# First residual formed during the scan and kept in HBM, second norm's scale and shift applied on ScalarE's evictions, and its residual added in the last stage

## The chip, the cores and the metric

One core of a Trainium2 chip runs the whole program in one launch. TensorE (PE), VectorE (DVE), ScalarE (ACT) and GpSimd (POOL) each work through a queue of their own in a fixed order; SyncE (SP) issues most of the DMAs. The metric is the device time of one execution in microseconds.

## What is computed

One layer of an encoder over 1024 positions of 1024 channels, in float32. A norm of x gives h. A projection of h feeds four mixers of 256 channels each: a state-space scan (S5), a matrix-state recurrence run forwards and backwards (RWKV-7), a gated convolution and a two-dimensional Fourier mixer. Their outputs are concatenated and projected, and two residuals with norms close the layer:

```
h = layer_norm(x, ln0_g, ln0_b)
mix = concat(s5(h), rwkv7(h), conv(h), fourier(h)) @ w_out
h = layer_norm(ALPHA * h + mix, ln1_g, ln1_b)
f = (silu(h @ w1) * (h @ w3)) @ w2
out = layer_norm(ALPHA * h + f, ln2_g, ln2_b)          # ALPHA = 2 ** 0.25
```

## The kernel before

Positions are eight tiles of 128, numbered 7 to 0 in the order in which they are worked on. Large products are made as three (`mm3`): each operand is split into a rounded upper part and the remainder, a cast on ScalarE and a subtraction on VectorE or GpSimd (`split_to`). `Tile` pools hand out buffers by tag, and a planner sets the order of each engine's queue from priorities and estimated times; an engine then takes its queue strictly in that order.

The stages, with their times in the profile: the first norm, the projection, S5 and the convolution (to about 440 us), with the preparation of the recurrence. `rk_scan` then makes 32 steps, 16 forwards and 16 backwards (about 497 to 675 us). Each direction needs the inverse of triangular blocks (`rk_inverse`): a loop of multiplications and sums that VectorE and GpSimd share by heads (L1174, L1176), then transposes and small products. The backward inverse runs beside the forward steps and has to be through before the first backward solve. A step of the scan goes through TensorE several times: transposes `pt`, products `px`, `pz`, `po` and `pc`, with ScalarE and VectorE evicting in between; L1321 is VectorE's update of the state, once in a step, and L1268 GpSimd's two copies for the step. Beside the steps stand the Fourier mixer (`fourier`, its table products `fpa` and `fpb` for each of two halves), `out_weights`, which loads the eight row blocks of w_out as `oraw` and splits them into `owa`, `owb`, `owc` (L1397 on VectorE, L1398 on GpSimd), and `rk_out`, which closes a tile of the recurrence (transposes `pgn`).

The output projection follows: for each tile t, `residual` loads x, subtracts the first norm's mean and multiplies by its deviation (L1432, VectorE), multiplies by ALPHA times the norm's scale row (L1434, GpSimd) and adds ALPHA times its shift row (L1435, VectorE), all 128x1024. `out_load` loads the mixers' output `yraw` from `d_y` and splits it; the products `ops` go through `out_product`, 48 for a tile, and L1455 adds them to the residual. `norm` makes the statistics (L172 and the lines to L187) and two instructions with the scale and shift rows (L1465, L1466). `turn` transposes two tiles (`ot`), evicts with two copies a tile (L1519), scales the tile by ALPHA on ScalarE (L1520), stores it in `d_acc`, and forms the sums and splits `H` that the feed-forward part's fast matrix scheme wants (L1528 to L1535, L1385). The first product of the feed-forward part (`fx`, `fy`, `fz`) runs from about 775 to 1238 us; weights are loaded, split and combined on the fly. The second (`ff_second`, products `f`) takes 924 products in seven groups to 1452 us; behind the fourth group (n == 3) it loads `d_acc` and adds it (L1782, L1783). `ff_out` makes the last norm.

Of the kernel before, what the change touches and what calls it, by code (L numbers as in the profile page):

```python
# [46 lines left out]
def pack(inp):  # L47
# [36 lines left out]
    for d, (m_in, m_st) in enumerate(((lo, st), (lo.T, st.T))):  # L84
# [5 lines left out]
        "x": f(a["x"][0]), "vec": f(vec), "rows": f(rows), "w_in": f(w_in), "lora": f(lora),  # L90
# [49 lines left out]
class Trunk:  # L140
# [72 lines left out]
    def build(self):  # L213
        tc = self.tc
        with tc.tile_pool(name="const", bufs=1) as cp, tc.tile_pool(name="dram", bufs=1, space=DRAM) as dp, \
# [4 lines left out]
            with tc.tile_pool(name="m", bufs=1) as m, tc.tile_pool(name="mp", bufs=1, space=PSUM) as pp:  # L220
                self.m, self.pp = m, pp
                with ExitStack() as pools:
# [3 lines left out]
                    def beside():  # L226
                        for part in (self.lora_project, self.rkv_project, self.conv, self.fourier_project):
                            yield from part()
                        self.far = [self.hp.tile([128, 4096], F32, tag=tag, name=tag + "f") for tag in ("HA0", "HB0", "HA1", "HB1")]
                        yield from self.until(("rows", 1, 1))  # L230
                        yield from self.first(self.rwkv_second(), 200000)
                        self.done.add("inverse")
                        yield from self.until("scan0")
                        yield from woven((self.fourier(), 0), (self.out_weights(), 32))
                        yield from self.out_first()
# [29 lines left out]
    def consts(self, cp):  # L265
# [37 lines left out]

        self.d_acc = self.dp.tile([8, 128, D], F32, name="d_acc")
# [675 lines left out]
    def rwkv_second(self):  # L980
# [3 lines left out]
        for c in (slice(8, 16), slice(0, 8)):  # L984
            for p in range(2):
                for i, dst in enumerate((self.av[1], self.bk[1])):
                    nc.sync.dma_start(out=dst[:, p, c], in_=self.d_p[p, i, :, c])
# [419 lines left out]


    def out_first(self):
        nc = self.nc  # L1410
        rows = self.t("TT", [128, 4, D], "rows")
        self.row4 = [rows[:, i] for i in range(4)]
        for i in range(4):
            self.row_load(rows[:, i], i)
        for i in range(2):
            nc.scalar.mul(out=rows[:, i], in_=rows[:, i], mul=ALPHA)
# [10 lines left out]

    def residual(self, t, tag):
        nc = self.nc
        ht = self.acc[t] = self.t(tag, [128, D], "acc")  # L1430
        nc.sync.dma_start(out=ht, in_=self.A["x"][t * 128:(t + 1) * 128, :])
        nc.vector.tensor_scalar(out=ht, in0=ht, scalar1=self.st0[:, t, 0:1], scalar2=self.st0[:, t, 1:2],  # L1432
                                op0=ALU.subtract, op1=ALU.mult)
        nc.gpsimd.tensor_tensor(out=ht, in0=ht, in1=self.row4[0], op=ALU.mult)  # L1434
        nc.vector.tensor_tensor(out=ht, in0=ht, in1=self.row4[1], op=ALU.add)  # L1435

    def out_load(self, t):
# [3 lines left out]
        self.split_to(*self.y_parts(t), raw, nc.vector if t > 5 else None)  # L1441
# [15 lines left out]
    def out_proj(self):  # L1457
        nc = self.nc
        g1, b1 = self.row4[2:]
        self.raws = ["WR", "T7"]  # L1460

        def norm(t):
            ht = self.acc[t]
            mean, rstd = self.row_stats(self.m, ht, D, LN_EPS)
            nc.vector.scalar_tensor_tensor(out=ht, in0=ht, scalar=mean, in1=g1, op0=ALU.subtract, op1=ALU.mult)  # L1465
            nc.vector.scalar_tensor_tensor(out=ht, in0=ht, scalar=rstd, in1=b1, op0=ALU.mult, op1=ALU.add)  # L1466
# [40 lines left out]
    def turn(self, j, tags):  # L1507
# [4 lines left out]
        for t, dst in ((7 - 2 * j, (b11, b21)), (6 - 2 * j, (b12, b22))):  # L1512
            ht = self.acc[t]
            for q in range(2):
# [4 lines left out]
                nc.scalar.copy(out=dst[q], in_=ps)  # L1519
            nc.scalar.mul(out=ht, in_=ht, mul=ALPHA)  # L1520
            nc.sync.dma_start(out=self.d_acc[t], in_=ht)
# [146 lines left out]
    def ff_second(self):  # L1668
# [9 lines left out]
        self.row_load(self.g2, 4)  # L1678
        self.row_load(self.b2, 5)
# [85 lines left out]
        for n in range(6):  # L1765
# [13 lines left out]
            if n == 3:  # L1779
                for t in range(NT - 1, -1, -1):  # L1780
                    x = self.ring("x", [128, D])
                    nc.sync.dma_start(out=x, in_=self.d_acc[t])  # L1782
                    tt(out=self.acc[t], in0=self.acc[t], in1=x, op=ALU.add)  # L1783

# [57 lines left out]
```

## Time and profile before

| | us |
|---|---|
| median of 3 runs | 1463.02 |
| runs | 1460.07 to 1464.85 |
| profiled execution | 1465.01 |
| its span | 1462.2 |
| granted TensorE clock, mean | 0.958 |

The profile is one execution. Its page gives busy times by engine over the whole span; the windows give them by stretch, and the chain of waits tells what released what. A busy TensorE is not TensorE at its peak. The prediction is made for the median; the profiled execution is 2.0 us above it.

### The profile page before, as it was taken

The numbers are of one execution on the slowest core, as the hardware profiler recorded it, in microseconds if no ns is written. First come the engines' busy times: TensorE is split into PE (matmuls) and PEld (weight loads), VectorE is DVE, ScalarE is ACT, GpSimd is POOL, SyncE is SP. The second block draws the span as 40 slices with busy tenths as digits, with TensorE's granted clock in tenths as the row PEclk, the third lists the DMA queues.
The fourth block names the chain that finished last, engine by engine and source line by source line (L and its number), as shares of the span: only waits on it lengthen the run. The fifth ranks groups of instructions, "written<-read, shape, count | busy, mean of one in ns | idle before, by whom it ended". The sixth has DMA issues, their size and how long they took to land.

```text
span 1462.2 us, 23749 instructions
## 1 busy us (share of the span) xinstructions
PE 1323.2 (90%) x9072; PEld 1196.4 (82%) x9072; DVE 1100.0 (75%) x1910; ACT 621.7 (43%) x1205; POOL 575.7 (39%) x524
## 2 busy tenths in 40 slices
PE   6968797977797999999877899999999999999997
PEld 5968787766796787877766899999999999888885
DVE  8997966487997685779999866666676665346888
ACT  4312141656324785761426544444444444332231
POOL 6466663153574332325567633333333331000006
PEclk9989998999899898999999899999999999999999
DMA  6111033122325004244312434444444438996752
GB/s 241 49 54 29 13 94 87 44 70 89 87 73 180 2 15 148 84 128 154 118 70 87 138 123 159 147 147 143 157 147 142 150 137 291 385 315 234 273 188 115
DMA packets 97056, 193.95 MB, mean 133 GB/s; under 512 B 24624, under 2 KB 50864, under 8 KB 96944
## 3 DMA queue, kind: packets, MB, share of 16 engines
q1 hardware_dynamic: 94912, 187.59, 38.3%
q10 hardware_dynamic: 2032, 4.86, 1.0%
q8 instruction: 71, 1.16, 0.3%
q14 instruction: 41, 0.34, 0.1%
HBM read 127.41 MB, written 63.96 MB: 131 GB/s over the span
## 4 chain that ended last, share of the span: by engine, by line
PE 42%; DVE 12%; DMA 3%; issue 2%; ACT 1%; POOL 1%; DVEq 0%; SPq 0%; ACTq 0%; POOLq 0%
PE fx L160 5%; PE fx L162 5%; PE fx L161 5%; PE f L160 4%; PE f L162 4%; PE f L161 4%; PE fy L162 2%; PE fy L160 2%; PE fy L161 2%; DVE acc L1435 1%; PE fz L160 1%; PE fz L161 1%; PE fz L162 1%; DMA fw<-w 1%; PE ops L161 1%
## 5 line engine op out<-in xcount | busy, mean ns | idle before, releaser
L160 PE MATMUL proj<-HA,wh 128*128 128x256 f32 x672 | 195.5, 291 | 14.6 <-DVE la L919 11.8
L160 PE MATMUL fx<-H,fc 128*128 128x256 f32 x704 | 196.9, 284 | 5.7 <-ACT fc L1384 2.2
L161 PE MATMUL proj<-HB,wh 128*128 128x256 f32 x672 | 200.1, 298 | 1.7 <-POOL HB L334 1.7
L162 PE MATMUL proj<-HA,wl 128*128 128x256 f32 x672 | 196.6, 293 | 4.1 <-POOL wl L394 4.1
L162 PE MATMUL fx<-H,fc 128*128 128x256 f32 x704 | 197.8, 282 | 2.6 <-DVE fc L1385 2.6
L1385 POOL TENSOR_TENSOR fc<-fw,fc 128x512 fp32r<-128x512 f32 x96 | 137.3, 1432 | 158.5 <-ACT fc L1384 157.7
L161 PE MATMUL fx<-H,fc 128*128 128x256 f32 x704 | 198.5, 282 | 0.0
L160 PEld LDWEIGHTS proj<-HA,wh 128*128 128x128 f32 x672 | 131.8, 196 | 18.4 <-issue 7.7
L162 PEld LDWEIGHTS proj<-HA,wl 128*128 128x128 f32 x672 | 131.5, 196 | 10.0 <-issue 5.5
L160 PEld LDWEIGHTS fx<-H,fc 128*128 128x128 f32 x704 | 132.5, 190 | 7.8 <-ACT fe L1633 2.7
L161 PEld LDWEIGHTS proj<-HB,wh 128*128 128x128 f32 x672 | 131.5, 196 | 7.0 <-issue 4.8
L162 PEld LDWEIGHTS fx<-H,fc 128*128 128x128 f32 x704 | 133.7, 191 | 2.8 <-DVE fc L1385 2.8
L161 PEld LDWEIGHTS fx<-H,fc 128*128 128x128 f32 x704 | 134.1, 191 | 0.1
L160 PE MATMUL f<-fb,fa 128*128 128x512 f32 x276 | 108.9, 395 | 0.0
L162 PE MATMUL f<-fb,fa 128*128 128x512 f32 x276 | 108.9, 394 | 0.0
L161 PE MATMUL f<-fb,fa 128*128 128x512 f32 x276 | 108.7, 394 | 0.0
L160 PE MATMUL fy<-H,fc 128*128 128x256 f32 x352 | 100.0, 284 | 4.7 <-ACT fe L1642 3.6
L162 PE MATMUL fy<-H,fc 128*128 128x256 f32 x352 | 99.5, 284 | 0.2 <-DVE fc L1385 0.2
L161 PE MATMUL fy<-H,fc 128*128 128x256 f32 x352 | 99.5, 283 | 0.0
L1821 POOL TENSOR_TENSOR acc<-acc,g 128x1024 f32<-128x1024 f32 x4 | 11.6, 2904 | 205.8 <-ACT acc L1820 205.8
L1384 ACT CAST fc<-fw 128x512 fp32r<-128x512 f32 x120 | 73.7, 619 | 31.8 <-POOL fc L1385 15.7
L1385 POOL TENSOR_TENSOR fc<-fs,fc 128x512 fp32r<-128x512 f32 x24 | 33.4, 1391 | 119.4 <-ACT fc L1384 116.0
(602 smaller groups left out, 3761.6 us busy)
## 6 DMA issues: line engine op xcount, KB each, us to landing
fa<-d_f SPq DMA_DIRECT2D x77, 512.0 KB, 3.8
d_f<-fg SPq DMA_DIRECT2D x70, 512.0 KB, 2.9
fw<-w SPq DMA_DIRECT2D x48, 512.0 KB, 3.6
fg<-w SPq DMA_DIRECT2D x44, 256.0 KB, 5.3
wraw<-w_in SPq DMA_DIRECT2D x16, 512.0 KB, 4.0
xt<-x SPq DMA_DIRECT2D x8, 512.0 KB, 8.1
oraw<-w_out SPq DMA_DIRECT2D x8, 512.0 KB, 3.7
yraw<-d_y SPq DMA_DIRECT2D x8, 512.0 KB, 4.1
```

Of the source, the lines that this page charges most:

```text
L160: mm(out, whi, xhi, start=start, stop=False, skip_group_check=shared)
L161: mm(out, whi, xlo, start=False, stop=False, skip_group_check=shared)
L162: mm(out, wlo, xhi, start=False, stop=stop, skip_group_check=shared)
L1384: nc.scalar.copy(out=hi, in_=raw)
L1385: (eng or nc.gpsimd).tensor_tensor(out=lo, in0=raw, in1=hi.bitcast(F32), op=ALU.subtract)
L1435: nc.vector.tensor_tensor(out=ht, in0=ht, in1=self.row4[1], op=ALU.add)
L1821: nc.gpsimd.tensor_tensor(out=o, in0=o, in1=self.g2, op=ALU.mult)
```

## The change

`residual` is cut to one load. A new generator, `residuals`, makes the same values for tiles 7 to 0 during the scan, woven with `fourier` and `out_weights`: it loads and scales the two rows on ScalarE's queue, then for each tile loads x on SP into the one buffer Z2, applies mean and deviation on ScalarE (Identity with scale and bias), multiplies and adds the rows on GpSimd and stores the tile in `d_res`. `issue_after` puts the first load behind the last of the loads by which the recurrence's rows return (L987).

`norm` becomes one VectorE instruction (subtract the mean, multiply by the deviation), and the tile is stored in `d_acc` from there, unscaled. `turn` evicts each 128x128 block by itself on ScalarE, with scale and shift per partition from `vec1`, and no longer scales the tile. In `ff_second` the rows g2 and b2 first hold ALPHA times the second norm's rows; behind the second group (n == 1) the normalized tile is loaded, multiplied by g2 on GpSimd, and it and b2 are added on VectorE; then the last norm's rows are loaded into the same buffers. The adds behind n == 3 go. The lower part of `yraw` is always made on VectorE, where GpSimd made it for six tiles.

```diff
-                        yield from woven((self.fourier(), 0), (self.out_weights(), 32))
+                        yield from woven((self.fourier(), 0), (self.residuals(), 0), (self.out_weights(), 32))
...
-                    nc.sync.dma_start(out=dst[:, p, c], in_=self.d_p[p, i, :, c])
+                    self.back = nc.sync.dma_start(out=dst[:, p, c], in_=self.d_p[p, i, :, c])
...
+    def alpha_row(self, out, i):
+        self.row_load(out, i)
+        self.nc.scalar.mul(out=out, in_=out, mul=ALPHA)
...
-        rows = self.t("TT", [128, 4, D], "rows")
-        self.row4 = [rows[:, i] for i in range(4)]
-        for i in range(4):
-            self.row_load(rows[:, i], i)
-        for i in range(2):
-            nc.scalar.mul(out=rows[:, i], in_=rows[:, i], mul=ALPHA)
...
+    def residuals(self):
+        nc = self.nc
+        g0, b0 = (self.t(f"Z{i}", [128, D], "row") for i in range(2))
+        self.alpha_row(g0, 0)
+        self.alpha_row(b0, 1)
...
+        for t in range(NT - 1, -1, -1):
+            x = self.t("Z2", [128, D], "res")
+
+            with self.tc.issue_after(self.back.ins):
+                nc.sync.dma_start(out=x, in_=self.A["x"][t * 128:(t + 1) * 128, :])
+            nc.scalar.activation(out=x, in_=x, func=AF.Identity, scale=self.st0[:, t, 1:2], bias=nm0[:, t:t + 1])
+            nc.gpsimd.tensor_tensor(out=x, in0=x, in1=g0, op=ALU.mult)
+            nc.gpsimd.tensor_tensor(out=x, in0=x, in1=b0, op=ALU.add)
+            nc.sync.dma_start(out=self.d_res[t], in_=x)
+            yield 8
+
     def residual(self, t, tag):
...
-        nc.sync.dma_start(out=ht, in_=self.A["x"][t * 128:(t + 1) * 128, :])
-        nc.vector.tensor_scalar(out=ht, in0=ht, scalar1=self.st0[:, t, 0:1], scalar2=self.st0[:, t, 1:2],
-                                op0=ALU.subtract, op1=ALU.mult)
-        nc.gpsimd.tensor_tensor(out=ht, in0=ht, in1=self.row4[0], op=ALU.mult)
-        nc.vector.tensor_tensor(out=ht, in0=ht, in1=self.row4[1], op=ALU.add)
+        self.acc[t] = self.t(tag, [128, D], "acc")
+        self.nc.sync.dma_start(out=self.acc[t], in_=self.d_res[t])
...
-        self.split_to(*self.y_parts(t), raw, nc.vector if t > 5 else None)
+        self.split_to(*self.y_parts(t), raw, nc.vector)
...
-            nc.vector.scalar_tensor_tensor(out=ht, in0=ht, scalar=mean, in1=g1, op0=ALU.subtract, op1=ALU.mult)
-            nc.vector.scalar_tensor_tensor(out=ht, in0=ht, scalar=rstd, in1=b1, op0=ALU.mult, op1=ALU.add)
+            nc.vector.tensor_scalar(out=ht, in0=ht, scalar1=mean, scalar2=rstd, op0=ALU.subtract, op1=ALU.mult)
+            nc.sync.dma_start(out=self.d_acc[t], in_=ht)
...
-                nc.scalar.copy(out=dst[q], in_=ps)
-            nc.scalar.mul(out=ht, in_=ht, mul=ALPHA)
-            nc.sync.dma_start(out=self.d_acc[t], in_=ht)
+
+                for k in range(4):
+                    nc.scalar.activation(out=dst[q][:, k], in_=ps[:, k, :], func=AF.Identity,
+                                         scale=self.vec1[:, 4 * q + k:4 * q + k + 1],
+                                         bias=self.vec1[:, 8 + 4 * q + k:9 + 4 * q + k])
...
-        self.row_load(self.g2, 4)
-        self.row_load(self.b2, 5)
+
+        self.alpha_row(self.g2, 2)
+        self.alpha_row(self.b2, 3)
...
-            if n == 3:
+            if n == 1:
                 for t in range(NT - 1, -1, -1):
                     x = self.ring("x", [128, D])
                     nc.sync.dma_start(out=x, in_=self.d_acc[t])
+                    tt(out=self.acc[t], in0=self.acc[t], in1=self.b2, op=ALU.add)
+                    nc.gpsimd.tensor_tensor(out=x, in0=x, in1=self.g2, op=ALU.mult)
                     tt(out=self.acc[t], in0=self.acc[t], in1=x, op=ALU.add)
+                self.row_load(self.g2, 4)
+                self.row_load(self.b2, 5)
```

The planner makes new queues of this. GpSimd's queue at the start of the backward steps, before: `oraw` is a loaded block of w_out, `owa` its lower part, the memset clears the state between the directions.

```order
L1198 COPY HA1f<-ua_4298 32x8x32 x4
L1268 COPY ring_4419<-HA1f 64x2x64 x4
L1398 TENSOR_TENSOR owa_5711<-oraw_5719,owa_5711 128x1024
L1398 TENSOR_TENSOR owa_5711<-oraw_5764,owa_5711 128x1024
L1319 MEMSET ring_4420 64x4x64
L1398 TENSOR_TENSOR owa_5711<-oraw_5790,owa_5711 128x1024
L1268 COPY ring_4419<-HA1f 64x2x64 x2
```

And now, where `res` is a tile of the residual, `row` one of its two rows:

```order
L1270 COPY ring_4420<-HA1f 64x2x64 x2
L1445 TENSOR_TENSOR res_6166<-res_6166,row_5406 128x1024
L1400 TENSOR_TENSOR owa_6098<-oraw_6106,owa_6098 128x1024
L1446 TENSOR_TENSOR res_6166<-res_6166,row_5407 128x1024
L1400 TENSOR_TENSOR owa_6098<-oraw_6132,owa_6098 128x1024
L1400 TENSOR_TENSOR owa_6098<-oraw_6219,owa_6098 128x1024
L1321 MEMSET ring_4421 64x4x64
```

The multiply and the add of tile 2 stand in front of the first and of the second block's subtraction.

VectorE's queue at the end of the backward inverse, before: L1174 and L1176 are the loop, L1187 and L1188 the transposes behind it, L1321 a step's state update (here its eleventh).

```order
L1174 TENSOR_TENSOR HA1f<-ua_4298,ti_4299 128x3x12
L1321 TENSOR_TENSOR ring_4420<-pc_5107,pl 64x4x64
L1176 TENSOR_TENSOR ti_4299<-ti_4299,HA1f 128x3x12
L1273 COPY ring_4418<-pt_421_5087 64x2x64
L1174 TENSOR_TENSOR HA1f<-ua_4298,ti_4299 128x2x12
L1290 TENSOR_TENSOR ring_4416<-px_5100,rkmask 128x4x64
L1176 TENSOR_TENSOR ti_4299<-ti_4299,HA1f 128x2x12
L1174 TENSOR_TENSOR HA1f<-ua_4298,ti_4299 128x12
L1176 TENSOR_TENSOR ti_4299<-ti_4299,HA1f 128x12
L1187 STREAM_TRANSPOSE tj_4623<-ti_4299 128x1024
L1188 STREAM_TRANSPOSE ua_4298<-ti_4299 128x1024
```

And now (two lines further down in the code: L1178 is the loop, L1189 and L1190 the transposes, L1323 the state update, here its thirteenth):

```order
L1275 COPY ring_4419<-pt_426_5129 64x2x64
L1178 TENSOR_TENSOR ti_4300<-ti_4300,HA1f 128x12
L1292 TENSOR_TENSOR ring_4422<-px_5142,rkmask 128x4x64
L1310 TENSOR_TENSOR ring_4418<-po_5156,ident 64x4x64
L1312 TENSOR_TENSOR ring_4418<-po_5156,rav_2860 64x2x64 x2
L1323 TENSOR_TENSOR ring_4421<-pc_5190,pl 64x4x64
L1275 COPY ring_4419<-pt_431_5170 64x2x64
L1189 STREAM_TRANSPOSE tj_4624<-ti_4300 128x1024
L1190 STREAM_TRANSPOSE ua_4299<-ti_4300 128x1024
L1292 TENSOR_TENSOR ring_4417<-px_5183,rkmask 128x4x64
```

The loop's end and the transposes stand two steps of the scan later.

TensorE's queue at the end of the scan, before: `pc` closes a step, `y7h` and `y7l` are the parts of tile 7 of the mixers' output.

```order
L160 MATMUL ops_6170<-owc_5713,y7h 128x512
L161 MATMUL ops_6170<-owc_5714,y7h 128x512
L1317 MATMUL pc_6193<-ring_4420,ring_4417 128x96 x3
L1373 MATMUL pgn_6044<-ident,yacc_4427 128x128
L1317 MATMUL pc_6193<-ring_4420,ring_4417 128x96
L162 MATMUL ops_6170<-owc_5713,y7l_6039 128x512
L160 MATMUL ops_6170<-owc_5715,y7h 128x512
```

And now:

```order
L1319 MATMUL pc_6143<-ring_4421,ring_4418 128x96 x4
L495 MATMUL fpb_5949<-tabs_5347,fzs_5354 128x512 x4
L1308 MATMUL po_6150<-ring_4417,ring_4416 128x128 x4
L1319 MATMUL pc_6159<-ring_4421,ring_4418 128x96 x4
L1375 MATMUL pgn_6027<-ident,yacc_4428 128x128
L1319 MATMUL pc_6196<-ring_4421,ring_4418 128x96 x4
L1375 MATMUL pgn_6027<-ident,yacc_4428 128x128
L1375 MATMUL pgn_6136<-ident,yacc_4428 128x128 x2
L1375 MATMUL pgn_6189<-ident,yacc_4428 128x128
L161 MATMUL ops_6270<-owa_6098,y7h 128x512
```

The first `ops` follows the last `pc`, and the second half of the Fourier mixer (`fpb`) stands in the last step but one, where the products of tile 7 were under way.

## Rows read from the trace of the kernel before

**Rows 1.** The page's line of busy times by engine: busy us, share of the span, instructions.

```profile
PE 1323.2 (90%) x9072; PEld 1196.4 (82%) x9072; DVE 1100.0 (75%) x1910; ACT 621.7 (43%) x1205; POOL 575.7 (39%) x524
```

**Rows 2.** Windows of 20 us over the end of the scan, the output projection and the start of the feed-forward part: stretch, busy us of PE, PEld, DVE, ACT, POOL with instructions in brackets, then the granted TensorE clock, the DMA share and GB/s.

```profile
520.00:540.00 20.00, 19.79 (x152) 17.01 (x152) 16.31 (x60) 15.41 (x46) 3.34 (x12) 1.00 0.00 1
...
680.00:700.00 20.00, 15.57 (x66) 11.56 (x65) 19.87 (x42) 4.21 (x8) 8.07 (x5) 0.93 0.37 111
...
740.00:760.00 20.00, 12.64 (x50) 9.71 (x49) 19.93 (x21) 5.42 (x9) 15.12 (x8) 0.83 0.16 53
...
780.00:800.00 20.00, 14.42 (x102) 13.64 (x103) 19.93 (x19) 13.96 (x26) 17.66 (x11) 0.91 0.32 123
...
860.00:880.00 20.00, 20.00 (x172) 20.00 (x171) 12.87 (x15) 8.56 (x16) 8.00 (x7) 1.00 0.27 90
```

**Rows 3.** The same columns for longer stretches: the output projection, the start of the feed-forward part, and most of its second product.

```profile
658.00:774.00 116.00, 101.71 (x458) 80.65 (x457) 109.41 (x164) 31.50 (x55) 63.33 (x33) 0.96 0.33 108
774.00:870.00 96.00, 81.27 (x622) 78.10 (x621) 81.52 (x104) 55.49 (x114) 58.80 (x39) 0.93 0.39 127
1240.00:1440.00 200.00, 200.00 (x862) 161.62 (x861) 131.29 (x216) 60.90 (x101) 11.15 (x5) 1.00 0.74 259
```

**Rows 4.** The chain of waits that ended last, from 650 to 870 us, in order of time: start us, us, what.

```profile
658.04 5.95 DMA acc<-x
...
670.59 3.06 DVE acc L1435
```

**Rows 5.** Groups by line with shapes kept apart, 655 to 865 us, VectorE: busy us in all, mean ns of one.

```profile
L1435 DVE TENSOR_TENSOR acc<-acc,rows 128x1024 f32<-128x1024 f32 x8 | 20.3, 2531 | 0.5 <-POOL acc L1434 0.5
L1466 DVE SCALAR_TENSOR_TENSOR acc<-acc,bnr,rows 128x1024 f32<-128x1024 f32 x8 | 16.0, 1995 | 0.2
L1465 DVE SCALAR_TENSOR_TENSOR acc<-acc,bnmv,rows 128x1024 f32<-128x1024 f32 x8 | 13.5, 1682 | 0.1
...
L1432 DVE TENSOR_SCALAR acc<-acc,st 128x1024 f32<-128x1024 f32 x8 | 7.4, 920 | 2.1 <-DMA acc<-x 2.1
```

**Rows 6.** The same view and stretch for GpSimd, then for ScalarE; the last row is ScalarE's 128x128 copy out of PSUM in the inverse, looked up by its line (min/median/max ns, first and last start us).

```profile
L1385 POOL TENSOR_TENSOR H<-hb,H 128x512 fp32r<-128x512 f32 x20 | 34.4, 1739 | 12.9 <-ACT H L1384 12.9
L1434 POOL TENSOR_TENSOR acc<-acc,rows 128x1024 f32<-128x1024 f32 x8 | 20.5, 2561 | 21.8 <-DVE acc L1432 14.3 <-DVE bnr L187 7.5
...
L1519 ACT COPY hb<-ot 128x512 f32<-128x512 f32 x16 | 9.0, 584 | 12.3 <-PE ot L1518 7.1 <-DVE TN L1374 5.1
L1520 ACT ACTIVATE acc<-acc 128x1024 f32<-128x1024 f32 x8 | 8.5, 1066 | 0.0
...
L1218 ACT COPY tn<-pm x6: 265/265/285, 467.9 to 568.9; 128x128 f32<-128x128 f32 x6
```

**Rows 7.** The timeline of VectorE and of GpSimd, first in the inverse of the forward scan (421 to 441 us), then in the output projection (669 to 675 us): start us, us, what; in square brackets the idle time before it.

```profile
430.55 2.48 DVE L1174 TENSOR_TENSOR tpr<-ua,ti 128x228 f32<-128x228 f32 x1
...
430.23 2.54 POOL L394 TENSOR_TENSOR wl<-wraw,wh 128x1024 fp32r<-128x1024 f32 x1
...
670.52 3.14 DVE L1435 TENSOR_TENSOR acc<-acc,rows 128x1024 f32<-128x1024 f32 x1
...
674.89 0.40 DVE L1321 TENSOR_TENSOR ring<-pc,pl 64x256 f32<-64x256 f32 x1
...
670.16 2.40 POOL L1434 TENSOR_TENSOR acc<-acc,rows 128x1024 f32<-128x1024 f32 x1 [2.38 <-DVE acc L1432]
674.78 2.37 POOL L1434 TENSOR_TENSOR acc<-acc,rows 128x1024 f32<-128x1024 f32 x1 [2.22 <-DVE acc L1432]
```

**Rows 8.** The state update that VectorE makes once in a step of the scan, looked up by its line in three stretches, one row each: count, min/median/max ns, first and last start us.

```profile
L1321 DVE TENSOR_TENSOR ring<-pc,pl x10: 408/417/417, 499.2 to 539.4; 64x256 f32<-64x256 f32 x10
...
L1321 DVE TENSOR_TENSOR ring<-pc,pl x12: 385/417/417, 579.6 to 645.7; 64x256 f32<-64x256 f32 x12
...
L1321 DVE TENSOR_TENSOR ring<-pc,pl x4: 403/408/411, 650.8 to 674.9; 64x256 f32<-64x256 f32 x4
```

**Rows 9.** The backward scan's inverse: the last of GpSimd's instructions in it, then the last of VectorE's and the last transposes of what follows it, from the timeline.

```profile
520.97 0.23 POOL L1176 TENSOR_TENSOR ti<-ti,HA1f 128x18 f32<-128x18 f32 x1
...
541.20 0.17 DVE L1176 TENSOR_TENSOR ti<-ti,HA1f 128x12 f32<-128x12 f32 x1
...
569.20 2.87 DVE L1223 STREAM_TRANSPOSE HB1f<-tn 32x512 f32<-32x512 f32 x4 [0.22 <-ACT tn L1218]
```

**Rows 10.** The chain of waits from 570 to 592 us, where the backward half of the scan starts.

```profile
575.81 4.99 POOL owa L1398 x2
...
580.82 3.87 DMA oraw<-w_out
...
589.74 1.06 PE pc L1317 x8
```

**Rows 11.** DMA issues of 640 to 700 us (KB each, median us to landing), then what reads the loaded rows of the mixers' output: min/median/max ns.

```profile
yraw<-d_y SPq DMA_DIRECT2D x6, 512.0 KB, 4.2
...
L1384 ACT CAST y7h<-yraw x1: 1047/1047/1047, 653.4 to 653.4; 128x1024 fp32r<-128x1024 f32 x1
L1385 DVE TENSOR_TENSOR y7l<-yraw,y7h x1: 1216/1216/1216, 654.7 to 654.7; 128x1024 fp32r<-128x1024 f32 x1
```

**Rows 12.** Groups by line of TensorE, the Fourier mixer's two table products: first 541.5 to 577.9 us, then 577.9 to 675.4 us.

```profile
L489 PE MATMUL fpa<-tabs,fzs 128*128 128x512 f32 x8 | 3.8, 593 | 0.0
...
L493 PE MATMUL fpb<-tabs,fzs 128*128 128x512 f32 x16 | 7.2, 592 | 0.0
```

More of the change, by code (lines that the diff above doesn't have):

```diff
@@ L89, in pack @@
     return {
-        "x": f(a["x"][0]), "vec": f(vec), "rows": f(rows), "w_in": f(w_in), "lora": f(lora),
+        "x": f(a["x"][0]), "vec": f(vec),
+        "vec1": f(np.concatenate([col(a["ln1_g"][0]), col(a["ln1_b"][0])], axis=1)), "rows": f(rows), "w_in": f(w_in), "lora": f(lora),
         "la2": f(la2), "g2": f(g2), "s5m": f(s5m), "s5d": f(a["s5_d"][0].T), "glu": f(a["s5_glu_w"][0]),
@@ L302, in consts @@
         self.d_p = self.dp.tile([2, 2, 128, 16, 2, 64], F32, name="d_p")
+        self.d_res = self.dp.tile([8, 128, D], F32, name="d_res")
         self.d_acc = self.dp.tile([8, 128, D], F32, name="d_acc")
@@ L1425, in out_first @@
         yield from self.out_product(7)
-    def residual(self, t, tag):
-        nc = self.nc
-        ht = self.acc[t] = self.t(tag, [128, D], "acc")
-        nc.sync.dma_start(out=ht, in_=self.A["x"][t * 128:(t + 1) * 128, :])
-        nc.vector.tensor_scalar(out=ht, in0=ht, scalar1=self.st0[:, t, 0:1], scalar2=self.st0[:, t, 1:2],
-                                op0=ALU.subtract, op1=ALU.mult)
-        nc.gpsimd.tensor_tensor(out=ht, in0=ht, in1=self.row4[0], op=ALU.mult)
-        nc.vector.tensor_tensor(out=ht, in0=ht, in1=self.row4[1], op=ALU.add)
+    def residuals(self):
[3 more added lines that the diff above has]
+        self.alpha_row(b0, 1)
+        self.vec1 = self.cp.tile([128, 16], F32, name="vec1")
+        nc.scalar.dma_start(out=self.vec1, in_=self.A["vec1"])
+        nm0 = self.cp.tile([128, NT], F32, name="nm0")
+        nc.vector.scalar_tensor_tensor(out=nm0, in0=self.st0[:, :, 0], scalar=-1.0, in1=self.st0[:, :, 1],
+                                       op0=ALU.mult, op1=ALU.mult)
+        for t in range(NT - 1, -1, -1):
[7 more added lines that the diff above has]
+            yield 8
+    def residual(self, t, tag):
+        self.acc[t] = self.t(tag, [128, D], "acc")
+        self.nc.sync.dma_start(out=self.acc[t], in_=self.d_res[t])
     def out_load(self, t):
@@ L1458, in out_proj @@
         nc = self.nc
-        g1, b1 = self.row4[2:]
         self.raws = ["WR", "T7"]
```

## The prediction, made before the changed kernel had run

> **What bounds the kernel now.** I read the profile from the whole to the place. Over the span TensorE is busy 90% and VectorE 75% [rows 1], but that is a mean over unlike stages, so I went to the windows next [rows 2]. In the backward scan's inverse (520 to 540 us) nobody is alone the bound: VectorE is busy 16.3 of 20 us and waits in turn for the others. In the output projection and the first 30 us of the feed-forward part VectorE is busy 19.9 of 20 us while TensorE falls to 12.6 to 15.6 and its granted clock to 0.83 to 0.93. From 860 us on TensorE is full. The long windows give the prize [rows 3]: from 658 to 774 us TensorE is idle 14.3 us and loses about 4.6 more to the clock (4% of 116), from 774 to 870 us it is idle 14.7 and loses 6.7. That is 40 us, and no edit of VectorE's work there can give back more. From 1240 to 1440 us TensorE is busy 200 of 200.
>
> The chain of waits says who holds the first of these stretches: x's load of 5.95 us, then the residual's adds on VectorE, one of them 3.06 us long [rows 4].
>
> **What leaves VectorE.** From 655 to 865 us the residual's two instructions and the norm's two cost 7.4 + 20.3 + 13.5 + 16.0 = 57.2 us [rows 5]. Added there are eight subtract-and-scale instructions of the new norm, priced like L1432 at 0.92, 7.4 us, and the lower parts of six tiles that move from GpSimd, at 1.22 each [rows 11], 7.3 us. VectorE sheds 42.5 us and GpSimd the residual's 20.5 [rows 6]. So (a) VectorE is no longer the bound of the projection. I let 5 of the 18.9 us stay, for tiles that still wait for each other: **-14**, bounds -19 and -4.
>
> **(b) What goes behind the scan.** The order of TensorE shows that the projection's 67 products which stood between the scan's last three steps now all come after its end. A product of this shape takes 200/862 = 0.232 us [rows 3], so **+15.5**, with a lower bound of 12 if some of it fills waits.
>
> **(c) The scan's last steps.** The state updates came 66.1/11 = 6.0 us apart until 645.7 us, and 24.1/3 = 8.0 us apart in the last three steps, with the products and the residual among them [rows 8]. Without both they fall to 6.0 (-6) or, as in the forward half with 40.2/9 = 4.5, to -10.5; but half the Fourier mixer now stands there, which could eat it all. I take **-7**.
>
> **(d) A new start.** The first product waits for the last Fourier half: a store and a load (4.2 each, pricing the store like the load), the cast 1.05 and the split 1.22 [rows 11], 10.7 us, of which the scan's last step covers some 6: **+5**, bounds 0 and 10.
>
> **(e) The feed-forward start.** Its 21.4 us of loss have a second source that stays: GpSimd's splits of H, 34.4 us [rows 6]. What goes is VectorE's backlog and one of two long instructions on the last tiles' way. I take **-9**, bounds -3 and -17.
>
> **(f) The backward scan's inverse.** The residual is not gone: eight multiplies and eight adds of GpSimd, 2.4 to 2.6 us each, now stand in the scan, four ahead of the inverse's loop and six in it. What such an instruction does to VectorE is seen in two places [rows 7]: an instruction of the inverse that met one took 2.48 us and ended 0.26 us after GpSimd's, and the residual's add that began 0.36 us into one took 3.14 and ended 1.10 after it. Both were held until GpSimd was through, some 2.0 us. But the state update, which reads PSUM, ran its usual 0.40 us inside one. So ten of them cost VectorE between 0 and 20 us, and VectorE has 18% idle there to give. VectorE's order puts the end of the loop behind the thirteenth step where it was behind the eleventh: two steps of 4.5, +9; in return one step fewer is left over behind the last transposes, -4.5. Then come two splits of the projection's weights, which with the load behind them were the chain there, 4.99 and 3.87 us [rows 10]; a residual's multiply now stands ahead of the first, +2.4. Together **+7**, bounds -2 and +20. GpSimd's own half of the loop ended 20 us ahead of VectorE's [rows 9], so six of its instructions (14.4 us) fit in.
>
> The Trainium skill ("SBUF — State Buffer", on the two separate sides) has a rule that speaks against this move: GpSimd and certain VectorE instructions, among them those with two SBUF inputs, take a shared port pair in turns, each for its whole length. The two held instructions agree with it.
>
> **(g) The Fourier mixer's first half.** Its two table products on TensorE were made about the wait for the inverse: 3.8 us and half of 7.2 [rows 12], 7.4 together. TensorE's order has them now six steps into the backward half, where each step waits on several engines. Bounds 0 and 7.4, **+5**.
>
> **(h) The rest of GpSimd's residuals.** Four more instructions stand among the backward steps, at most 4 x 2.4 = 9.6 us. Most of VectorE's work there reads PSUM: **+2**.
>
> **(i) Edits at nothing.** ScalarE loses 16 copies and 8 scalings, 9.0 + 8.5 us, and gets 64 scaled copies of 128x128, which at 0.265 (the nearest of this size) are 17.0 [rows 6]; a quarter of 0.584 each would be 9.3. ScalarE is over half idle there [rows 3] and hides either; if not, a tile's turn is some 1 us longer. In the second product of the feed-forward part eight more adds on VectorE and eight multiplies on GpSimd come in: VectorE is busy 131 of 200 us and GpSimd 11 while TensorE is full [rows 3], and the order lets the adds in one or a few at a time between splits that run ahead: 0, or up to 4 if the splits run dry. On SP the early loads of x wait for the store before them in the one buffer; ahead of the tables' load they delay only work that (g) has already. Rows that were loaded and scaled on ScalarE's queue at 640 us are now made at the kernel's start, among waits: 0.
>
> **The sum.** -14 + 15.5 - 7 + 5 - 9 + 7 + 5 + 2 = +4.5 us on the profiled execution of 1465.0. That lies 2.0 above the median of the three runs, so I set the change against the median: **1467 us**. A measurement of this kernel tells about 0.3% (4.4 us) from no change, so this is at the edge of no change; with the middle terms off by a few us it runs from 1458 to 1476.
>
> **Rivals.**
> *The relief comes through.* The inverse and the Fourier half hide in waits as the residual did not: (f) to (h) come to 2, (c) is -8, (d) +3 and (e) -12. -14 + 15.5 - 8 + 3 - 12 + 2 = -13.5: 1449 us, between 1438 and 1458. For it: VectorE's 18% idle in the inverse and the slack of 20 us on GpSimd. Against it: the loop's end stands two steps later in the very order.
> *VectorE is held by GpSimd in the scan.* Its place is the inverse's loop, whose instructions read SBUF alone; its price is 2.0 us for each of the sixteen, 32 us, less 18% that VectorE has idle, 26 in place of the 9 of (f) and (h): +21.5, 1484 us. It decides once more than about half of them meet such an instruction. For it: both rows that show a meeting. Against it: the state update that ran free. The rule of the Trainium skill named under (f), taken for every one of the sixteen, is this case.
> *GpSimd waits for x.* Each residual needs load, scaling, multiply, add, store in one buffer, 4.2 + 1.1 + 2.4 + 2.4 + 4.2 = 14.3 us, and GpSimd's queue stands still where the load is late. With three waits of 5.3 us and 14.4 us of work its half of the loop passes its slack of 20 us by 10: +14.5, 1477 us. Against it: the slack is passed only if all three loads are late.
>
> **Chances.** The sum 0.38 (0.05 of it faster, 0.22 the same, 0.11 slower), relief 0.33 (0.31 faster, 0.02 the same), held by GpSimd 0.21 and the wait for x 0.08, both slower. Faster 0.36, same 0.24, slower 0.40. Both signs are likely, so the likeliest case keeps its own range, 1458 to 1476, and the range for 8 in 10 runs from the middle of the relief, 1446, to just beyond the held case, 1486, leaving about a tenth on each side.
>
> **What would show it.** (a): TensorE's idle time in the 116 us behind the scan falls below 8 us and VectorE's busy share below 0.85. (b), (d): no product before the last step, then a gap of about 5 us. (c): the last three state updates about 6 us apart. (f): the loop's last instruction on VectorE at 545 to 552 us; above 555 the held case, at 541 the relief. Instructions of the inverse longer than 2 us would show the holding. (g): two table products inside one step of the backward half. (e): TensorE full some 90 us after the last product, not 95. I would be wrong outright if the feed-forward part's second product showed gaps on TensorE, or if the time before 440 us moved.

## The result, and the profile after

| | median, us | runs | ratio to the kernel before (95%) |
|---|---|---|---|
| kernel before | 1462.41 | 4, 1460.07 to 1464.85 | |
| change | 1483.28 | 4, 1482.47 to 1488.19 | 1.0147 [1.0122, 1.0172] |

The change is slower by 1.5%, 16 us above the forecast of 1467, near the upper end of the range of 1446 to 1486. The profiled execution took 1482.47 us, 17.5 more than the one before, of which 18.0 lie in the span.

Page, busy us, share of the span, instructions, against [rows 1]:

```profile
PE 1323.1 (89%) x9072; PEld 1196.3 (81%) x9072; DVE 1106.7 (75%) x1901; ACT 641.1 (43%) x1255; POOL 595.4 (40%) x534
```

The totals tell nothing: TensorE does the same work and VectorE's total is even a little higher. The windows do. First 20 us each, against [rows 2]: the backward inverse, the gap behind the scan, the projection, the feed-forward start.

```profile
520.00:540.00 20.00, 15.08 (x109) 12.56 (x109) 19.25 (x47) 13.68 (x39) 12.18 (x20) 0.94 0.25 84
680.00:700.00 20.00, 7.36 (x28) 5.43 (x29) 13.36 (x31) 2.71 (x4) 4.66 (x5) 0.66 0.83 249
740.00:760.00 20.00, 20.00 (x96) 16.43 (x95) 13.52 (x23) 11.48 (x26) 5.67 (x5) 1.00 0.43 138
800.00:820.00 20.00, 16.60 (x118) 15.31 (x116) 17.65 (x15) 18.64 (x45) 18.26 (x11) 0.91 0.12 40
```

Then the long stretches, against [rows 3]: from the scan's last step (it ends at 682) to the last product of the projection, from there to where TensorE is full, and in the second product.

```profile
676.00:789.00 113.00, 99.85 (x450) 80.20 (x449) 73.56 (x137) 33.31 (x71) 27.99 (x19) 0.94 0.40 128
789.00:888.00 99.00, 84.08 (x632) 80.82 (x631) 81.68 (x104) 59.80 (x137) 58.74 (x40) 0.93 0.33 107
1255.00:1455.00 200.00, 200.00 (x871) 161.97 (x870) 155.72 (x224) 62.98 (x105) 30.13 (x12) 1.00 0.76 268
```

In the middle of the projection the relief is there: VectorE is busy 13.5 of 20 us where it was full, and TensorE 20.0 of 20 where it was at 12.6. But the inverse has VectorE at 19.25 of 20 (16.3 before), TensorE stands still for most of 680 to 700 us, and the start of the feed-forward part looks as it did: VectorE is busy 81.7 us in the second stretch, as against 81.5. The second product is full as before.

Counted from the starts of single instructions in both traces, the difference lies thus (600th: the 600th product of the feed-forward part; differences are taken before rounding):

| stretch, us | before | after | difference |
|---|---|---|---|
| start to first backward solve (`pz`) | 575.7 | 589.3 | +13.6 |
| of it, up to the last `pre` of the recurrence's preparation | 403.6 | 407.8 | +4.2 |
| to the scan's last `pc` | 100.6 | 93.1 | -7.5 |
| scan's last `pc` to last `ops` | 97.4 | 106.9 | +9.6 |
| of it, up to the first `ops` | none: 67 came ahead of the scan's end | 12.7 | |
| to the 600th `fx`, `fy`, `fz` | 97.2 | 99.1 | +2.0 |
| 600th to the first `f` | 358.1 | 358.4 | +0.3 |
| first `f` to last `f` | 223.0 | 223.0 | 0.0 |

**Before the scan.** 4.2 of the 13.6 us are lost before 408 us, ahead of every residual instruction. TensorE's waits for a VectorE instruction of the projection (`la`), 140 to 190 us (us in all, times, longest), before and after:

```profile
PE proj L160 <- DVE la L919: 6.9, 1, 6.9
PE proj L161 <- DVE la L921: 14.6, 1, 14.6
```

VectorE's queue has the third `la` behind more of S5's instructions: it starts at 168.3 us where it started at 160.4. So it is in all ten runs below that form the residual in the scan (168.2 to 169.2, the last `pre` at 407.6 to 410.1), and not in `e1` and `e11`, which don't (160.6 and 160.8, the last `pre` at 401.8 and 402.2). It comes with the residual's half of the change; which of its lines moves the queue was not told apart.

**The inverse.** VectorE's timeline in the loop, start us, us, what; then GpSimd's over the same time, against [rows 7, 9]:

```profile
530.09 2.40 DVE L1176 TENSOR_TENSOR HA1f<-ua,ti 128x204 f32<-128x204 f32 x1
533.00 2.38 DVE L1176 TENSOR_TENSOR HA1f<-ua,ti 128x192 f32<-128x192 f32 x1
...
552.08 2.18 DVE L1176 TENSOR_TENSOR HA1f<-ua,ti 128x72 f32<-128x72 f32 x1
...
560.71 0.15 DVE L1178 TENSOR_TENSOR ti<-ti,HA1f 128x12 f32<-128x12 f32 x1
```

```profile
529.84 2.43 POOL L1445 TENSOR_TENSOR res<-res,row 128x1024 f32<-128x1024 f32 x1
532.70 2.46 POOL L1446 TENSOR_TENSOR res<-res,row 128x1024 f32<-128x1024 f32 x1
551.80 2.38 POOL L1445 TENSOR_TENSOR res<-res,row 128x1024 f32<-128x1024 f32 x1 [0.74 <-ACT res L1444]
```

Each of the three VectorE instructions starts 0.25 to 0.30 us into one of GpSimd's and ends 0.22 us (530.09 + 2.40 against 529.84 + 2.43), 0.22 and 0.08 us after it. One of about this size that meets none of these takes half a us (128x220 at 527.09: 0.49). Over the loop's sixty instructions VectorE was busy 17.9 us before and 28.9 after; six now last over 1 us, one for each of the six residual instructions inside. The loop starts at 505.2 where it started at 496.8 and ends at 560.9 where it ended at 541.4: it lasts 11.1 us longer, as much as VectorE's busy time in it grew.

The Trainium skill ("SBUF — State Buffer", the section on the two separate sides) says that a VectorE instruction with two SBUF inputs and a GpSimd instruction that reads SBUF take a shared port pair by an exclusive lock, whoever starts first holding it for its whole length. The six agree with it.

**The gap.** The chain of waits behind the scan's last step, and one row of SP's waits from 676 to 700 us (us in all, times, longest):

```profile
684.05 0.73 POOL TN L1378
684.80 4.48 DMA d_y<-TN
689.30 0.36 SPq L1359
689.75 4.22 DMA yraw<-d_y
694.04 1.05 ACT y7h L1386
695.13 0.79 PE ops L161
```

```profile
SPq L1359 <- DMA d_y<-TN: 3.4, 2, 2.5
```

The first product reads `y7h`, cast from the rows loaded at 689.75. That load is the second in SP's queue there, and stands behind a load for the next `rk_out` (L1359, into the buffer `TN` that the last store reads). SP waits for the landing of a store made 2 us after the scan's end, so nothing of store, load and cast is covered by the scan. The Fourier mixer's own store, issued at 679.45, took 6.6 us and let SP's first load of `yraw` go at 686.14, 3.6 us ahead of this one: without `rk_out`'s store an estimated 9 of the 12.7 us would have stayed.

**The last steps.** VectorE's state updates, against [rows 8]: 5.0, 5.7 and 6.8 us apart, where the last three took 24.1 in all.

```profile
663.53 0.41 DVE L1323 TENSOR_TENSOR ring<-pc,pl 64x256 f32<-64x256 f32 x1
668.49 0.41 DVE L1323 TENSOR_TENSOR ring<-pc,pl 64x256 f32<-64x256 f32 x1
674.21 0.42 DVE L1323 TENSOR_TENSOR ring<-pc,pl 64x256 f32<-64x256 f32 x1 [0.60 <-PE pc L1319]
681.01 0.42 DVE L1323 TENSOR_TENSOR ring<-pc,pl 64x256 f32<-64x256 f32 x1
```

### The profile page after: what moved, and what is told of

It is laid out like the page before. It is cut to its first block, busy times and chain, and to the rows that moved or that the text cites. A ratio compares the mean times of both kernels' runs of the same rounds, so it can differ in the third digit from the quotient of the medians.

```text
span 1480.2 us, 23836 instructions
## 1 busy us (share of the span) xinstructions
PE 1323.1 (89%) x9072; PEld 1196.3 (81%) x9072; DVE 1106.7 (75%) x1901; ACT 641.1 (43%) x1255; POOL 595.4 (40%) x534
## 4 chain that ended last, share of the span: by engine, by line
PE 60%; DVE 24%; ACT 6%; issue 4%; DMA 4%; POOL 2%; SPq 1%; DVEq 0%; POOLq 0%; ACTq 0%
PE fx L163 5%; PE fx L161 5%; PE fx L162 5%; PE f L161 4%; PE f L163 4%; PE f L162 4%; PE fy L161 2%; PE fy L162 2%; PE fy L163 2%; PE ops L161 2%; PE ops L162 2%; PE ops L163 2%; PE pc L1319 2%; PE proj L161 1%; PE proj L163 1%
## 5 line engine op out<-in xcount | busy, mean ns | idle before, releaser
L161 PE MATMUL fy<-H,fc 128*128 128x256 f32 x352 | 99.1, 282 | 1.6 <-ACT fe L1660 1.3
L1386 ACT CAST fb<-fs 128x512 fp32r<-128x512 f32 x47 | 29.1, 623 | 92.2 <-PE f L163 59.0
```

The lines of the kernel that those rows point to most:

```text
L161: mm(out, whi, xhi, start=start, stop=False, skip_group_check=shared)
L1386: nc.scalar.copy(out=hi, in_=raw)
```

## The experiments

The theory after this result had three parts: the relief of VectorE is real; it is lost to work placed late (the Fourier mixer, and with it all products of the projection); and GpSimd's residuals hold VectorE. The rival: placement matters little, and the holding, or something new in the feed-forward start, makes the whole loss. Each run stands beside runs of the kernel before on the same chip; times are medians in us.

### The two halves of the change apart

`e1_norm_only` forms the residual as before.

```diff
-woven((self.fourier(), 0), (self.residuals(), 0), (self.out_weights(), 32))
+woven((self.fourier(), 0), (self.out_weights(), 32))
```

> Only the second norm's part of the change: one VectorE instruction, scale and shift on ScalarE's evictions, its residual added in the feed-forward part's second product; the first residual is made as before, in the output projection. Theory A (the loss is made in the scan and at the projection's start, where the first residual's new place pushes the Fourier mixer and the first 67 products back): faster than before, 1445 to 1458 us, with products still among the scan's last steps. Rival B (the loss is in the turn: 64 small evictions where there were 16, and no gain at the feed-forward start): slower than before, 1468 us or more.

Measured: 1466.85 against 1464.93, ratio 1.0013 [1.0003, 1.0023]. Neither number came. The norm's half alone brings nothing. VectorE's groups by line, 655 to 790 us (busy us, mean ns of one):

```profile
L1442 DVE TENSOR_TENSOR acc<-acc,rows 128x1024 f32<-128x1024 f32 x8 | 15.1, 1893 | 0.0
...
L1386 DVE TENSOR_TENSOR H<-yraw,H 128x1024 fp32r<-128x1024 f32 x4 | 7.5, 1872 | 0.0
L1386 DVE TENSOR_TENSOR y<-yraw,y 128x1024 fp32r<-128x1024 f32 x3 | 6.6, 2211 | 0.0
```

The lower parts of `yraw`, now on VectorE, take 1.87 and 2.21 us where one took 1.22 [rows 11]. Three of the seven run beside one of GpSimd's multiplies, which are still in the projection here, and take 1.6 to 3.4; part of the saving is eaten.

`e2_residual_only` moves the residual into the scan and leaves norm, `turn` and second product as before (the rest of the diff undone).

> Only the first residual's part of the change: made in the scan and kept in HBM; the second norm as before. Theory A: at least as slow as the whole change, 1483 to 1495 us, since the norm's 29.5 us stay on VectorE. Rival B: near the time before, 1460 to 1470 us.

Measured: 1490.71 against 1464.93, 1.0177 [1.0161, 1.0193]. As expected: the loss is all in the residual's half.

### Placement and GpSimd, a table of four

In `woven` the generator with the least time so far goes next, and what each yields is also handed to the planner as time of the work beside the scan. Each tile's `yield 8` therefore places everything behind it, Fourier and projection, later against the scan's steps.

`e3_no_gpsimd` keeps that and drops GpSimd's two instructions, so that the residual lacks the first norm's rows:

```diff
-            nc.gpsimd.tensor_tensor(out=x, in0=x, in1=g0, op=ALU.mult)
-            nc.gpsimd.tensor_tensor(out=x, in0=x, in1=b0, op=ALU.add)
```

> The whole change, but GpSimd's multiply and add of each tile of the first residual are left out, so the residual lacks the first norm's scale and shift rows; loads, ScalarE's scaling and stores stay, and so does the late place of the Fourier mixer. Theory A (late products and a late start): little is won, 1473 to 1481 us. Rival C (VectorE is held by GpSimd's sixteen instructions in the scan): most of the loss is gone, 1459 to 1466 us.

Measured: 1473.78 against 1464.93, 1.0061 [1.0043, 1.0079]: at the lower end of theory A's range, and far from C's. The scan ends 18.8 us earlier than in the change, but 9.8 of them come back behind it: the gap grows from 12.7 to 21.0 us.

`e4_weave_free` keeps GpSimd and lets the residuals count no time:

```diff
-            yield 8
+            yield 0
```

> The whole change, but the generator of the residuals yields 0 instead of 8 for each tile, so that the planner's weaving counts no time for it: the Fourier mixer's table products come back to where they stood before (scan steps 14 and 23) and 77 products come before the scan's end, while GpSimd's sixteen instructions keep their places in the queue. Theory A: most of the loss is gone, 1460 to 1470 us, and the gap at the projection's start closes. Rival C: 1478 to 1485 us, the loop of the inverse as late as in the change.

Measured: 1468.66 against 1464.93, 1.0022 [1.0013, 1.0032]. 77 products stand ahead of the scan's end again, and there is no gap. So the time is A's, though C's sign came too: the loop of the inverse ends at 562.5. The first two of the long windows above, here (the scan ends at 700.4):

```profile
658.00:776.00 118.00, 114.99 (x604) 94.72 (x604) 90.99 (x207) 48.63 (x114) 30.02 (x29) 1.00 0.43 141
776.00:875.00 99.00, 82.93 (x636) 79.26 (x635) 82.45 (x104) 59.27 (x136) 58.45 (x39) 0.95 0.34 111
```

TensorE is idle 3.0 of the 118 us and its granted clock is 1.00: the relief of the projection, whole. It is paid for ahead of this: the first backward solve comes at 596.8.

`e5_no_gpsimd_free` does both edits (like `e3`, its residual lacks the norm's rows).

> e4 with GpSimd's multiply and add of the first residual left out (the residual lacks the first norm's rows); loads, ScalarE's scaling and stores stay, the Fourier mixer stands at its old place. Theory A' (the change's loss has two parts, the late Fourier mixer and GpSimd's sixteen instructions in the scan, each hiding a part of the other): with both gone the scan ends 15 to 25 us earlier than in e4 and the time is 1438 to 1452 us. Rival D (the end is set behind the projection, by the feed-forward start, whatever the scan does): 1460 to 1468 us.

Measured: 1448.49 against 1463.54, 0.9904 [0.9882, 0.9927]. The scan ends at 683.5, 16.9 ahead of e4. The four, as ratio and in us of 1464:

| | GpSimd's sixteen in | out | their cost |
|---|---|---|---|
| residuals count 8 each | +1.47%, +21.5 (the change) | +0.61%, +8.9 (e3) | 12.6 |
| residuals count 0 | +0.22%, +3.2 (e4) | -0.96%, -14.1 (e5) | 17.3 |
| cost of the counted time | 18.3 | 23.0 | |

So with both costs out, the change's idea is worth 14 us, with the 4 us before the scan still lost; the counted time costs 18 to 23, GpSimd's instructions 13 to 17. The latter is more than the holding: without them the planner also makes other queues (in `e3` and `e5` the loop's end stands behind nine state updates, in the change and `e4` behind twelve). Neither cause makes the whole loss alone.

### Is it the holding, or GpSimd's time?

`e6_short_gpsimd` is e4 with each residual instruction in four pieces, more GpSimd work in shorter holds:

```diff
+            for c in range(4):
+                s = slice(256 * c, 256 * c + 256)
+                nc.gpsimd.tensor_tensor(out=x[:, s], in0=x[:, s], in1=g0[:, s], op=ALU.mult)
+                nc.gpsimd.tensor_tensor(out=x[:, s], in0=x[:, s], in1=b0[:, s], op=ALU.add)
```

> e4 with each of GpSimd's 128x1024 instructions of the first residual cut into four of 128x256, the same values. If VectorE (and the queue behind) loses by being held through one long instruction, shorter holds let it in between: the first backward solve comes 5 to 10 us earlier than in e4 (596.8 us), 1456 to 1464 us. If the amount of GpSimd's work or the wait for x is what costs: 1466 to 1473 us, with no earlier solve.

Measured: 1455.68 against 1463.54, 0.9952 [0.9936, 0.9968]: 0.70% (10.2 us) below e4, just under its range, and 0.5% faster than the kernel before. GpSimd's row by line (min/median/max ns), and the longest instruction of VectorE's loop:

```profile
L1447 POOL TENSOR_TENSOR res<-res,row x32: 718/724/1177, 468.4 to 614.4; 128x256 f32<-128x256 f32 x32
```

```profile
533.98 0.83 DVE L1178 TENSOR_TENSOR ti<-ti,HA1f 128x192 f32<-128x192 f32 x1
```

Four pieces take 2.9 us where one took 2.4 (48.8 against 38.8 us in all), yet VectorE's loop falls from 28.9 us busy in e4 to 23.5, its longest instruction from 2.40 to 0.83, and the first solve comes 7.3 us earlier. More GpSimd time and less loss: it isn't the amount of GpSimd's work, and in the loop it is the length of the hold that costs. Cutting gives back 10.2 of the 17.3. The pieces also let GpSimd's copies for the scan's steps (L1270) stand between them; but from 496 to 600 us the profile of e4 shows no engine waiting for one of those. How much of the rest is the planner's new queue (the loop starts behind three state updates, in e4 behind two) was not told apart.

`e11_before_short` cuts L1434 of the kernel before in four in the same way.

> The kernel before with GpSimd's multiply of the residual (L1434) cut into four of 128x256, nothing else. If short holds alone, not the change, made e6 faster than before: 1453 to 1458 us. If e6's gain comes from the work that left the projection: 1461 to 1465 us.

Measured: 1462.83 against 1463.88, 0.9996 [0.9987, 1.0005]. Short holds alone don't make e6's gain; it belongs to the residual in the scan.

### Why the feed-forward start did not move

Its stretch, last `ops` to the 600th product, was 97.2 us before and 99.1 after, and 98.9 in e4. Five runs look for its bound. `e7_two_evictions` is e4 with `turn`'s evictions as two copies a tile (the second norm's scale and shift are left out of the feed-forward input):

```diff
-                for k in range(4):
-                    nc.scalar.activation(out=dst[q][:, k], in_=ps[:, k, :], ...)
+                nc.scalar.copy(out=dst[q], in_=ps)
```

> e4 with the turn's evictions made as two copies of 128x512 a tile, as before; the second norm's scale and shift are left out of the feed-forward part's input. If the 64 small evictions are what takes back VectorE's relief at the feed-forward start: the stretch from the last product of the projection to the 600th of the feed-forward part falls from 98.9 to 95 us or less, 1462 to 1465 us. If not: 98 us or more, 1467 to 1470 us.

Measured: 1469.00 against 1463.54, 1.0048 [1.0029, 1.0067]; the stretch 99.9. The small evictions alone aren't it.

`e8_turn_on_vector` is e4 with all of `turn`'s splits on VectorE:

```diff
-        put(1, b21, nc.gpsimd)
+        put(1, b21, nc.vector)
...
```

> e4 with the turn's splits of H all made on VectorE, where GpSimd makes five of seven. If the feed-forward start is slow because GpSimd's splits hold VectorE: that stretch falls from 98.9 to below 93 us, 1455 to 1463 us. If it is slow because VectorE has too much to do: it grows to 103 us or more, 1472 us or more.

Measured: 1460.43 against 1463.54, 0.9988 [0.9974, 1.0002]; the stretch 94.9, GpSimd busy 44 of 95 us there. The time is in the range of the first case, but the stretch is some 4 us shorter, between what the two have for it.

`e9_short_turn_vector` joins e6 and e8.

> e6 and e8 together: the change, uncounted in the weave, GpSimd's residual in pieces of 128x256, all splits of the turn on VectorE. If the two gains lie in different stretches (the scan, the feed-forward start), they add: the projection ends near 763 us, the 600th product comes 95 us later, 1447 to 1453 us. If the feed-forward start only gives back what came late: 1454 to 1457 us, as e6.

Measured: 1457.28 against 1463.88, 0.9955 [0.9942, 0.9968], the stretch 97.9: as e6. The two gains don't add, so e8's 4 us aren't a steady gain of this stretch.

`e10_short_splits` is e6 with GpSimd's 128x512 subtractions of `turn` and of the weights cut in two:

```diff
+        if eng in (None, nc.gpsimd) and hi.shape[1] == 4:
+            for c in (slice(0, 2), slice(2, 4)):
+                nc.gpsimd.tensor_tensor(out=lo[:, c], in0=raw[:, c], in1=hi[:, c].bitcast(F32), op=ALU.subtract)
+            return
```

> e6 with GpSimd's 128x512 subtractions of the turn and of the feed-forward part's weights cut into two of 128x256. If the feed-forward start is slow because VectorE is held through whole GpSimd instructions: the stretch from the last product to the 600th falls from 95.5 to 90 us or less, 1445 to 1452 us. If it is VectorE's own amount of work, or GpSimd's: 95 us or more, 1455 to 1460 us.

Measured: 1453.56 against 1463.88, 0.9938 [0.9923, 0.9953], between the two ranges and not told apart from e6 (0.9952 [0.9936, 0.9968]). The stretch is 95.3, as in e6, which is the second case's sign: holding through these instructions isn't its bound.

`e12_no_lower_h` is e6 without `turn`'s 28 subtractions (the products read the upper part in place of the lower):

```diff
-            self.split_to(H[i][:, 0, j % 2], H[i][:, 1, j % 2], x, eng)
+            nc.scalar.copy(out=H[i][:, 0, j % 2], in_=x)
```

> e6 with the turn's 28 subtractions left out (H's lower parts are not made; the products read the upper part in their place, so that TensorE's work stays). If VectorE's and GpSimd's work at the feed-forward start is what that stretch lasts for: from the last product of the projection to the 600th it falls from 95.5 to 88 us or less, 1443 to 1449 us. If it is the last tiles' chain of steps, with the clock, whatever these two engines do: 93 us or more, 1452 to 1457 us.

Measured: 1449.00 against 1464.03, 0.9894 [0.9873, 0.9914]. The stretch in e6 and in e12, in windows from each one's last `ops` to its 600th product:

```profile
762.80:858.30 95.50, 78.95 (x625) 76.94 (x624) 81.06 (x104) 56.83 (x128) 59.57 (x40) 0.96 0.36 113
```

```profile
763.70:856.10 92.40, 79.90 (x630) 76.49 (x629) 63.87 (x99) 59.31 (x136) 41.04 (x30) 0.98 0.37 117
```

VectorE loses 17.2 us of work and GpSimd 18.5, and the stretch falls by 3.1, to 92.4. The time is at the edge of the first case's range, the stretch nearer the second's. So it is mostly not the amount of work on these two. But another engine fills up when they are relieved. The first 30 us, e6 and then e12 (the fourth busy time is ScalarE's):

```profile
762.80:792.80 30.00, 20.08 (x150) 18.97 (x148) 29.72 (x31) 24.94 (x58) 25.09 (x17) 0.94 0.17 53
```

```profile
763.70:793.70 30.00, 24.87 (x190) 22.64 (x189) 19.53 (x31) 29.66 (x73) 12.19 (x10) 1.00 0.23 71
```

ScalarE, with the casts of `H` and the evictions, is busy 29.7 of 30 us in e12. `e7` relieved ScalarE there (20.0 of 30), but with VectorE full (29.8 of 30). Relief of both at once was not run, so that the two bind this start in turn stands as an untested case.

## Why the prediction was off, step by step

The sum against the stretches of the two profiled executions:

| step | forecast | measured | from |
|---|---|---|---|
| (a) VectorE no longer the bound | -14 | -18.6 | (a), (b) and (d) together are +9.6; less 15.5 and 12.7 |
| (b) products behind the scan | +15.5 | +15.5 | 0 products ahead of its end; 67 at the forecast's price, not timed apart |
| (d) new start | +5 | +12.7 | the gap |
| (c), (g), (h) backward half | 0 | -7.5 | 93.1 against 100.6 |
| (f) to the first backward solve | +7 | +13.6 | 589.3 against 575.7; 4.2 of it before 408 us |
| (e) feed-forward start | -9 | +2.0 | 99.1 against 97.2 |
| (i) second product | 0 | 0.0 | 223.0 in both |
| sum | +4.5 | +17.7 | |

**The step that failed is (e)**: 11 us, where the sum is 13 off and the other misses nearly cancel. It took VectorE's backlog and one long instruction for what makes the start slow. The row it rested on, VectorE full from 780 to 800 us, was right, and so was the loss. But the change takes little from VectorE in this stretch: the work leaves the projection (73.6 of 113 us busy where it was 109.4 of 116), while here its busy time stays (81.7 us against 81.5 in the long windows), and TensorE is idle 14.9 of 99 us as it was 14.7 of 96. And where VectorE was relieved of 17.2 us (e12), only 3.1 came of it; the stretch stays within 92 to 103 us in all kernels run here. e7, e8, e10 and e12 exclude the small evictions, the holding, and the amount of work on VectorE and GpSimd, each taken alone, as the main cause. What is left, ScalarE and VectorE in turn, the last tiles' way through norm, transposes and splits, and the granted clock of 0.91 to 0.98, was not told apart.

**(d) was undersized** by 8 us. Store, load and cast were the right chain with the right prices (4.48, 4.22 and 1.05 against 4.2, 4.2 and 1.05), but not hidden: the store that came last is `rk_out`'s, not the Fourier mixer's, and SP's queue puts the load behind it. The Fourier mixer's store itself took 6.6 us and not the load's 4.2.

**(f) and (h) were undersized**, and the cover of the backward half hid that. (f)'s +7 is +9, -4.5 and +2.4 from the queue's order, with the holding, which it bounded at 20, at nothing because VectorE had 18% idle; in the loop the holding made 11.0 us, and the loop grew by as much. (f)'s sign that the holding is real came as written: the loop ended above 555, with instructions over 2 us. The order was misread a little too: in the queue printed above the prediction the loop's last instruction stands behind the twelfth state update, one step later than before, and only the transposes stand behind the thirteenth. Without GpSimd's instructions (e3) the first solve comes at 581.9 and the backward half takes 81.7 us: so of (f)'s 13.6 they made 7.4, and 11.4 of the backward half, where (h) had 2. Most of what is left of the 13.6 is the 4.2 before 408 us. The rest of the backward half, (c) and (g), fell by 18.9, where -2 was forecast; the last three steps gave 6.6 of it, as (c) had it. Two table products in one step, as (g) had it, didn't come: at 668.8 and 674.0 they stand in two.

**A sign of being wrong outright came.** The prediction named two: gaps in the second product, which didn't come, and a move of the time before 440 us, which did, by 4.2 us. No term of the sum priced a new order of the queues that early; only (i) looked there, and it put the rows now made at the kernel's start at nothing.

**(a) and (b)** held, and so did (i) behind the scan. (a) came near its bound of -19, by this reckoning: what is idle behind the scan, 13.2 of 113 us, is the gap of (d), and VectorE's share is 0.65.

**The rivals.** The held case gave 1484, and 1483 came; its own sign, a loop end above 555, came. But its sum was not what happened: it had 26 us for the sixteen, and the table of four shows 13 to 17. The rest is the relief that (e) didn't bring, the gap and the 4.2 us before 408. So it is luck in part that its number came, and with it that the time lies in the range at all: the range reached to 1486 for this case's sake. The relief's -13.5 exists as a number: -14.1 in e5, once the counted time and GpSimd's rows are both gone. It too came by another sum: from the scan's last `pc` to the last `ops` e5 takes 75.9 us where it was 97.4, while the feed-forward start is 1.6 us shorter, not 12. The wait for x was not seen as a cause: GpSimd's half of the loop did lose its slack, ending 0.8 us after VectorE's, but GpSimd waited only 2.0 us there for a scaled x (500 to 565 us); the rest are the residual instructions among the loop's own and its waits for the scan's steps.

## What to carry to other kernels

A time that a generator counts for itself in a planned weave is a cost like an instruction: here eight yields of 8 put 67 products behind the scan's end and half a mixer into its last steps, for 18 to 23 us. Work handed to GpSimd beside a VectorE loop that reads two SBUF operands was priced here by the length of its instructions, not by GpSimd's free time; cut into pieces it cost less. Relief of a full engine is counted in the stretch that the work leaves, and only up to the next bound: before a stretch's loss is booked as gain, see what the engine sheds in it and what else is late there. And where a planner makes the queues, compare the two traces from their start, not only around the edit.

## What the runs showed of the hardware

- A 128x256 two-input instruction on GpSimd took 0.72 us (median) against 2.35 for 128x1024: 26% more time in all (48.8 against 38.8 us), 0.70% less for the kernel (e6 against e4).
- ScalarE's 128x128 eviction with scale and shift per partition took 0.476 us, where the forecast had 0.265 from a plain copy of that size [rows 6]; with two plain copies a tile in their place the time did not fall (e7):

```profile
L1537 ACT ACTIVATE hb<-ot,vec x64: 450/476/547, 720.3 to 811.5; 128x128 f32<-128x128 f32 x64
```
